# The third chunk's schedule of a hybrid encoder step, written out product by product

## The chip, the cores and the metric

The kernel runs on one core of a Trainium2 chip. A core has five engines, each with a queue of its own: TensorE (PE in the profile; its weight loads are PEld), VectorE (DVE), ScalarE (ACT), GpSimd (POOL) and SyncE (SP), which here does nothing but issue DMA transfers. An engine takes the instructions of its queue in order, so an instruction that waits holds up everything behind it. A semaphore tells an engine that another one, or a transfer, has finished. The metric is device time in microseconds for one execution, smaller is better; several runs are made, and their median counts.

## The reference

One layer of an encoder is applied to 1024 prompt frames and 32 sample frames, with model width 1024. With `rmsnorm` ahead of each part, and residual adds:

1. Mixers: `z = rmsnorm(x) @ w_in` is cut into q, k, v, three convolution inputs and two gates. One mixer is sliding-window attention with 16 heads, the other a gated convolution of width 3. `x += (sigmoid(ga) * (attn @ w_attn_out) + sigmoid(gb) * (conv @ w_conv_out)) @ w_mix_out`.
2. Cross attention with 4 heads into 256 memory tokens: `x += attn(rmsnorm(x) @ w_cq, K_mem, V_mem) @ w_co`.
3. MLP with hidden width 4096: `x += relu(rmsnorm(x) @ w_up)**2 @ w_down`, then a last `rmsnorm`.

The outputs are the two activations and the new key, value, convolution and memory states. Everything is in fp32.

## The kernel before

**Number format.** Each fp32 operand is split into a high part and a low part of a type that TensorE reads fast: ScalarE casts the high part, VectorE subtracts to get the low part (`split`, lines 128 to 130). A product is then three matmuls: high by high, high by low, low by high (`gemm`, L193 to L195; `product`, L864 to L866, for one half of the contraction). Weights come as tiles of 128 x 1024 (512 KB): `fetch_w` (L155) loads one, `issue_w` casts and splits it, two weights ahead of their use. For a weight whose key is in `kept`, the low half is stored to DRAM at the first use (`wl_d`, L172) and loaded at the next ones (L166) in place of the subtraction.

**Chunks and halves.** Features lie on partitions, frames along the free axis. Parts 1 and 2 treat the 1056 frames in three chunks of 384, 384 and 288. The MLP treats them in two halves of 528, each of two quarters of 264, and uses a scheme with seven products in place of eight for 2 x 2 blocks; so it needs sums and differences of weight blocks and of activation blocks. A first part of the MLP's up product, the "first-half products" (`up_one` for one quarter, `up_two` for both), needs only the first half of the frames: `xa[0]` for quarter 0 and `xa[1]` for quarter 1, the latter with its last 144 frames from the second chunk.

**Order of work.** The program is a list, `plan`, of items: functions with the weights that they take. A tile scheduler then orders the instructions on each engine by a timeline that it simulates; those marked `pin` keep their order. The main stages are: 32 hosts (input projections, each with a unit of window attention beside it, `hosts`), the attention output products (`do_attn_out`), the gates (`gate_pair`), then for each chunk eight `do_conv_out` and eight `do_mix` products with the steps of cross attention beside them, then the MLP.

**Sums of weights.** `sum_step` (L702) works on a list of 50 pieces. A step issues from GpSimd's queue the load of one piece (L712, L714) into one of two tiles in turn (`ws`, `xacc`), adds the blocks of the piece of the step before (four additions, L719), and stores the result to DRAM (L723, L725). All of it is pinned. Before the change a step goes with the hosts 3, 5, 7, 9, 11 and each from 12 on (25 steps), one with the first gate, three with each of the eight attention output products. `after_gates` gives the room of `ws` to the tiles M of the merged mixers. `do_conv_out` adds on GpSimd (L1050) after a multiplication on VectorE (L1049); its work tiles and many others share six `ct` slots.

**The third chunk.** The product list of the third chunk (`trunks[2]`, 16 products) runs with the statistics of the first chunk's MLP norm, the cross attention of the second chunk (`cross_steps(1)`: `mem_load_s`, statistics, the query products `do_cq`, six lists of head work from `cross_units`, the output products `do_co`) and `normed(0, f)` beside it, spread by `beside` with one step behind each product. Behind it comes `open_first`, which opens on the room of the M tiles the pool with the Z slots and the `lt` slots. A second list of 32 items follows: `up_one` for weights 0 to 5 in quarter 0, the same in quarter 1, and twenty halves of `up_two`; `then(i, ...)` puts steps behind item i of it. `normed(c, f)` (L1278) makes one normed block and stores it to DRAM (`xn_d`, L1281); `second_load` (L1299) fetches quarter 1 from there, `second_split` (L1293, L1294) splits it. `chunk_col` and `chunk_row` make the norm's statistics as a column and as a row R.

**The activation sums.** `open_sums` loads 16 raw blocks from `xn_d`. `comb_sums(k)` (L1371 to L1383), for k from 0 to 3, forms differences in `xacc`, copies them over the raw blocks by DMA, and splits `t2`. `up_ready` loads sums of weights into the tiles `s31` and `s24`. `up_start` and 16 times `up_pair` follow; in the first `up_pair` the blocks b22 and n4 are split (`comb_split`) before the difference `h22` (L1477).

Of the kernel before, what the change touches and what calls it, by code (L numbers as in the profile page):

```python
# [18 lines left out]
P = 128  # L19
# [21 lines left out]
def hybrid_step(ctx: ExitStack, tc: tile.TileContext, io):  # L41
# [693 lines left out]
    for i, h in enumerate(hosts):  # L735
# [278 lines left out]

    m_cm = mpool = cr_cm = cr = None

    def after_gates():
# [201 lines left out]

    L, S = {}, {}  # L1220
# [33 lines left out]
    def zslot(dt=F32R):  # L1254
        return S["z"].tile([P, HT], dt, tag="Z", bufs=8, name=nm("Z"))

    def lslot(dt=F32):
        return S["z"].tile([P, HT], dt, tag="lt", bufs=6, name=nm("lt"))

# [16 lines left out]
    def normed(c, f):  # L1276
        t = tmp(CH[c][1])
        pin(dve.scalar_tensor_tensor(t, x1[c][f], col(G_MLP + f), R[c], op0=ALU.mult, op1=ALU.mult))  # L1278
        for h, to, at in in_halves(c):
            if c < 2 or f > 3:  # L1280
                sp.dma_start(xn_d[h][:, f, to], t[:, at])  # L1281
        if c == 2:
            sp.dma_start(raw("n1" if f < 4 else "n3", f % 4)[:, HT - CH[c][1] :], t)
# [6 lines left out]
    def split_here(hi, lo):  # L1290
# [16 lines left out]
    def put(*args):  # L1307
        later.append(args)
# [6 lines left out]
    def up_one(i, q):  # L1315


        def fn(w):
            flush()
            a, b = (acc_tile([P, QT]) for _ in range(2))  # L1320
            s, h = lslot(), lslot()
            product(a, w, 0, xa[q][:4], True)
            s, h = s[:, :QT], h[:, :QT]
            act.copy(s, a)
            put(quarter(s1_d[:, i], q), s)
            product(b, w, 1, xa[q][4:], True)
            dve.tensor_add(h, b, s)
            dve.scalar_tensor_tensor(h, h, 0.0, h, op0=ALU.max, op1=ALU.mult)
            put(quarter(op_d["b11"][:, i], q), h)
# [40 lines left out]

    def comb_sums(k):  # L1371
        n3, n1 = xacc[0][:, :HT], xacc[0][:, HT:]
        t2 = L["pool"].tile([P, 1024], F32, tag="wr2", bufs=2, name=nm("t2"))[:, :HT]
        pin(dve.tensor_sub(n3, raw("n1", k), raw("n3", k)))
        sp.dma_start(raw("n3", k), n3)
        pin(dve.tensor_sub(t2, raw("t2", k), n3))
# [3 lines left out]
        pin(act.copy(hi, t2))  # L1380
        pin(dve.tensor_sub(lo, t2, hi.bitcast(F32)))
# [79 lines left out]
    def up_pair(i):  # L1461
# [18 lines left out]
        squared_relu(h22)  # L1480
        put(op_d["b22"][:, i], h22)
        if last:
            pump2(4)
# [147 lines left out]
    normeds = lambda c, at: [(at + f, lambda f=f: normed(c, f)) for f in range(NF)]  # L1631
    left = beside(left + cross_steps(1), trunks[2], normeds(0, 2))
    assert not left
# [12 lines left out]
    call = lambda fn, *args: lambda: item(lambda: fn(*args))  # L1646
    then(0, call(chunk_col, 1))
    then(1, call(chunk_row, 1), call(chunk_col, 2))
    for f in range(NF):
        then(2 + f // 4, call(normed, 1, f))  # L1650
    then(2, call(chunk_row, 2))
    then(3, lambda: item(do_cq(2, 0), ("w_cq", 0)))
    then(4, lambda: item(do_cq(2, 1), ("w_cq", 1)))
    for f in range(NF):
        then(4, call(second_load, f))
        then(5, call(second_split, f))
    for i, (_, calls) in zip((5, 7, 9, 10, 12, 14, 15), cross_units(2)):
        then(i, *[call(x) for x in calls])
    then(16, call(open_sums))
    then(17, lambda: item(do_co(2, 0), ("w_co", 0)))  # L1660
    then(18, lambda: item(do_co(2, 1), ("w_co", 1)))
    then(19, call(open_late), call(chunk_col, 2))
    then(20, call(chunk_row, 2))
    then(21, call(xacc_tile))
    for f in (0, 4, 1, 5, 2, 6, 3, 7):
        then(21, call(normed, 2, f))
    for k in range(4):
        then(23 + k, call(comb_sums, k))
    then(27, call(up_second, 0))
    then(28, call(comb_split, "n1"))  # L1670
    assert len(fillers) == 32
    for i, filler in enumerate(fillers):
# [273 lines left out]
```

## Time and profile before

| | |
|---|---|
| median of 3 runs | 1784.36 us (1780.86 to 1791.03) |
| the profiled execution | 1793.09 us, its span 1791.3 us |
| TensorE busy | 1735.8 us (97%) |
| VectorE, ScalarE, GpSimd busy | 1175.1, 853.9, 580.5 us |
| mean granted TensorE clock | 0.988 |
| SyncE's DMA queue, GpSimd's DMA queue | 306.32 MB, 52.60 MB |
| HBM read, written | 257.08 MB, 97.34 MB |

The span runs from the first to the last instruction. Views are told by what they are: the page has the totals, 40 slices of the span with busy tenths, and the costliest groups; the windows view has the busy time of each engine in chosen stretches; the waits view has who waited for whom; the view in order of time has start, duration, engine, line, operation, output and inputs, and in brackets the idle time before and what ended it. An engine's name with a q behind it is its sequencer, which issues DMAs.

### The profile page before, as it was taken

What the parts mean: (1) busy time and instruction counts of PE and PEld (TensorE: products, weight loads), DVE (VectorE), ACT (ScalarE), POOL (GpSimd) and SP (SyncE); (2) the same over time, 40 slices, a digit from 0 to 9 for tenths busy, and PEclk for the clock granted to TensorE, in tenths of its full rate; (3) what the DMA queues carried; (4) which work ended last, traced back from release to release, by engine and by line L of the source; (5) the groups of instructions that cost most, each with busy time, mean ns of one, the idle gap of its engine ahead of it and who ended that gap; (6) DMA issues with size and microseconds to landing.
All of it is one profiled execution on the core that took longest, in us unless ns stands there. A gap on an engine that the chain in (4) does not pass through costs nothing.

```text
span 1791.3 us, 32530 instructions
## 1 busy us (share of the span) xinstructions
PE 1735.8 (97%) x12250; PEld 1717.5 (96%) x12250; DVE 1175.1 (66%) x2221; ACT 853.9 (48%) x1646; POOL 580.5 (32%) x655
## 2 busy tenths in 40 slices
PE   8999999999999999997999988999999999999998
PEld 8999999999999999996899987999999999999998
DVE  6776767868666747554667775557666686556575
ACT  8643534435345334333556664655444463433443
POOL 0023145653453444453215140014555510100121
PEclk9999999999999999998999999998999999999999
DMA  5332234344346888766765768787766686554554
GB/s 181 101 112 92 87 104 153 118 145 144 134 151 239 289 297 279 269 239 239 245 230 193 251 241 290 254 289 237 228 220 221 214 297 218 179 187 167 191 176 159
DMA packets 186684, 360.98 MB, mean 202 GB/s; under 512 B 19216, under 2 KB 103984, under 8 KB 186400
## 3 DMA queue, kind: packets, MB, share of 16 engines
q1 hardware_dynamic: 171472, 306.32, 50.6%
q0 software_dynamic: 15056, 52.60, 8.2%
q8 instruction: 96, 1.57, 0.4%
q14 instruction: 60, 0.49, 0.1%
HBM read 257.08 MB, written 97.34 MB: 198 GB/s over the span
## 4 chain that ended last, share of the span: by engine, by line
PE 73%; DMA 13%; POOL 7%; DVE 3%; issue 2%; ACT 1%; SPq 0%; DVEq 0%; ACTq 0%; POOLq 0%
PE acc L193 10%; PE acc L195 10%; PE acc L194 10%; PE acc L1733 6%; PE acc L1732 6%; PE acc L1731 6%; DMA wsum_d<-ws 3%; PE acc L864 3%; PE acc L866 3%; PE acc L865 3%; DMA wsum_d<-xacc 3%; POOL ws L719 3%; POOL xacc L719 3%; PE pc L866 2%; PE pc L865 2%
## 5 line engine op out<-in xcount | busy, mean ns | idle before, releaser
L129 ACT CAST wh<-wr 128x1024 fp32r<-128x1024 f32 x217 | 227.8, 1050 | 415.9 <-PE acc L1732 125.7
L130 DVE TENSOR_TENSOR wl<-wr,wh 128x1024 fp32r<-128x1024 f32 x217 | 283.3, 1306 | 143.3 <-ACT wh L129 142.0
L193 PE MATMUL acc<-X,wh 128*128 128x384 f32 (+1 forms) x864 | 282.3, 327 | 7.6 <-ACT wh L129 7.6
L194 PE MATMUL acc<-X,wh 128*128 128x384 f32 (+1 forms) x864 | 279.4, 323 | 0.0
L195 PE MATMUL acc<-X,wl 128*128 128x384 f32 (+1 forms) x864 | 278.8, 323 | 0.3 <-DVE wl L130 0.3
L269 POOL TENSOR_TENSOR xacc<-xacc,ct 128x384 f32<-128x384 f32 (+1 forms) x56 | 74.1, 1328 | 414.2 <-ACT ct L267 404.2
L193 PEld LDWEIGHTS acc<-X,wh 128*128 128x128 f32 x864 | 163.2, 189 | 8.3 <-ACT wh L129 7.6
L194 PEld LDWEIGHTS acc<-X,wh 128*128 128x128 f32 x864 | 163.6, 189 | 0.6
L195 PEld LDWEIGHTS acc<-X,wl 128*128 128x128 f32 x864 | 163.1, 189 | 0.9 <-DVE wl L130 0.8
L193 PE MATMUL acc<-Y,wh 128*128 128x384 f32 (+1 forms) x432 | 139.9, 326 | 12.8 <-DVE ct L1049 12.8
L195 PE MATMUL acc<-Y,wl 128*128 128x384 f32 (+1 forms) x432 | 140.0, 325 | 3.2 <-DMA wl<-wl_d 3.1
L194 PE MATMUL acc<-Y,wh 128*128 128x384 f32 (+1 forms) x432 | 140.0, 325 | 0.6 <-DVE Y L775 0.6
L1733 PE MATMUL acc<-n,wl 128*128 128x264 f32 x352 | 100.0, 284 | 0.0
L1731 PE MATMUL acc<-n,wh 128*128 128x264 f32 x352 | 100.0, 284 | 0.0
L1732 PE MATMUL acc<-n,wh 128*128 128x264 f32 x352 | 100.0, 284 | 0.0
L129 ACT CAST PTh<-pt 128x512 fp32r<-128x512 f32 (+3 forms) x94 | 46.1, 517 | 109.5 <-PE pt L582 107.5
L719 POOL TENSOR_TENSOR ws<-ws 128x256 f32<-128x256 f32 x100 | 94.2, 942 | 5.7
L193 PEld LDWEIGHTS acc<-Y,wh 128*128 128x128 f32 x432 | 81.5, 189 | 13.2 <-ACT wh L129 13.1
L719 POOL TENSOR_TENSOR xacc<-xacc 128x256 f32<-128x256 f32 x100 | 86.9, 869 | 5.5
L195 PEld LDWEIGHTS acc<-Y,wl 128*128 128x128 f32 x432 | 81.6, 189 | 4.2 <-DMA wl<-wl_d 3.7
L194 PEld LDWEIGHTS acc<-Y,wh 128*128 128x128 f32 x432 | 81.6, 189 | 1.1 <-DVE Y L775 1.1
L864 PE MATMUL acc<-n,wh 128*128 128x264 f32 x256 | 72.7, 284 | 1.0 <-DVE Z L1477 1.0
(398 smaller groups left out, 5512.2 us busy)
## 6 DMA issues: line engine op xcount, KB each, us to landing
wr<-in_w_in SPq DMA_DIRECT2D x53, 512.0 KB, 4.0
wr<-in_w_up SPq DMA_DIRECT2D x52, 512.0 KB, 4.9
wr<-wsum_d SPq DMA_DIRECT2D x40, 512.0 KB, 3.4
wl<-wl_d SPq DMA_DIRECT2D x26, 512.0 KB, 4.8
wr<-in_w_conv_out SPq DMA_DIRECT2D x24, 512.0 KB, 4.3
wr<-in_w_mix SPq DMA_DIRECT2D x24, 512.0 KB, 4.2
wr<-in_w_down SPq DMA_DIRECT2D x24, 512.0 KB, 3.7
n_d<-Z SPq DMA_DIRECT2D x32, 264.0 KB, 4.6
```

What stands on the lines that cost most here:

```text
L129: act.copy(hi, src)
L130: dve.tensor_sub(lo, src, hi.bitcast(F32))
L193: pe.matmul(out, wh[:, a], hi, start=(k == 0), stop=False)
L194: pe.matmul(out, wh[:, a], lo, start=False, stop=False)
L195: pe.matmul(out, wl[:, a], hi, start=False, stop=(k == len(acts) - 1))
L719: pin(pool_e.tensor_tensor(t[:, to], t[:, x], t[:, y], op=ALU.add))
L864: pe.matmul(acc, wh[:, a], hi, start=(start and k == 0), stop=False, skip_group_check=True)
L865: pe.matmul(acc, wh[:, a], lo, start=False, stop=False, skip_group_check=True)
L866: pe.matmul(acc, wl[:, a], hi, start=False, stop=(k == 3), skip_group_check=True)
L1731: pe.matmul(a, wh[:, s], hi, start=(t == 0 and k == 0), stop=False, skip_group_check=True)
L1732: pe.matmul(a, wh[:, s], lo, start=False, stop=False, skip_group_check=True)
L1733: pe.matmul(a, wl[:, s], hi, start=False, stop=(t == 1 and k == 7), skip_group_check=True)
```

## The change

Six things change.

- Hosts 4, 6, 8 and 10 get a `sum_step` too (29 steps in the host stage).
- The two lists become one of 48 items: 0 to 7 the third chunk's `do_conv_out`; then its eight `do_mix` with first-half products of quarter 0 at items 10, 13 and 16 between them; 19 to 21 the other three of quarter 0; 22 to 27 those of quarter 1; 28 to 47 `up_two`. All steps beside them are written out with `then`, and `open_first` stands behind item 18, the last mix product. The first three first-half products take their results' tiles from the cross pool.
- The low halves of the six `w_up` weights are no longer kept in DRAM, and for the third chunk neither are those of `w_cq` and `w_co`: VectorE computes them.
- Quarter 1's operands: `second_load` is gone. `open_first` loads the 120 frames of the first chunk from `xn_d`, and `normed(1, f)` copies the 144 frames of the second chunk from its tile.
- `comb_sums` becomes `sums_first` and `sums_then`, the second called one item later; k = 1 uses the tiles `s31` and `s24`, and `up_ready(0)` follows behind it.
- In the first `up_pair`, the splits of b22 and n4 go behind the stores of `h22` and of the last product.

```diff
-        if i % 2 and i > 1 or i > 11:
+        if i % 2 and i > 1 or i > 3:
             extras.append((1, sum_step))
...
     def open_first():
         closed(m_cm)
-        S["z"] = ctx.enter_context(tc.tile_pool(name="first", bufs=1, reuse_waits="tile"))
+        S["l"] = ctx.enter_context(tc.tile_pool(name="first", bufs=6, reuse_waits="tile"))
+        S["z"] = ctx.enter_context(tc.tile_pool(name="second", bufs=8, reuse_waits="tile"))
+        for f in range(NF):
+            z = zslot()
+            xa[1][f] = (quarter(z, 0), quarter(z, 1))
+            sp.dma_start(xa[1][f][1].bitcast(F32)[:, : CH[0][1] - QT], xn_d[0][:, f, QT : CH[0][1]])
+        for name in ("w_cq", "w_co"):
+            del kept[name, 1]
...
     def open_late():
...
-        up_ready(0)
...
     def normed(c, f):
...
+        if c == 1:
+            sp.dma_start(xa[1][f][1].bitcast(F32)[:, CH[0][1] - QT :], t[:, : HT - CH[1][0]])
...
-    def second_load(f):
-        z = zslot()
-        xa[1][f] = (quarter(z, 0), quarter(z, 1))
-        sp.dma_start(xa[1][f][1].bitcast(F32), xn_d[0][:, f, QT:])
...
     def up_one(i, q):
...
-            s, h = lslot(), lslot()
+            if q == 0 and i < 3:
+                s, h = (cr.tile([P, QT], F32, tag=t, bufs=2, name=nm(t)) for t in ("us", "uh"))
+            else:
+                s, h = lslot()[:, :QT], lslot()[:, :QT]
...
-    def comb_sums(k):
-        n3, n1 = xacc[0][:, :HT], xacc[0][:, HT:]
+    def sums_first(k):
+        if k == 1:
+            n3, n1 = (L["pool"].tile([P, 1024], F32, tag=t, name=nm(t))[:, :HT] for t in ("s31", "s24"))
+        else:
+            n3, n1 = xacc[0][:, :HT], xacc[0][:, HT:]
...
+        pin(act.copy(comb["t2", k][0], t2))
+
+    def sums_then(k):
+        t2 = t2s.pop(k)
         hi, lo = comb["t2", k]
-        pin(act.copy(hi, t2))
         pin(dve.tensor_sub(lo, t2, hi.bitcast(F32)))
...
-        if i == 0:
-            comb_split("b22")
-            comb_split("n4")
         h22 = lt()
...
         put(op_d["b22"][:, i], h22)
+        if i == 0:
+            comb_split("b22")
...
+        if i == 0:
+            comb_split("n4")
         if not last:
             m2 = sums()
...
-    left = beside(left + cross_steps(1), trunks[2], normeds(0, 2))
-    item(open_first)
-    kept.update((("w_up", UP[i][0]), None) for i in range(NQ))
-    fillers = [up_one(i, q) for q in range(2) for i in range(NQ)]
+    ones_q = [up_one(i, q) for q in range(2) for i in range(NQ)]
+    mixes = trunks[2][NF:]
+    fillers = trunks[2][:NF] + mixes[:2]
+    for i in range(3):
+        fillers += [ones_q[i]] + mixes[2 * i + 2 : 2 * i + 4]
+    fillers += ones_q[3:]
...
+    then(0, *[call(x) for x in left[0][1]], call(mem_load_s))
+    then(1, call(chunk_stats, 1))
+    then(2, *[lambda j=j: item(do_cq(1, j), ("w_cq", j)) for j in range(2)])
     for f in range(NF):
+        then(2 + f, call(normed, 0, f))
+    for i, (_, calls) in zip((3, 5, 7, 9, 11, 12), cross_units(1)):
+        then(i, *[call(x) for x in calls])
+    then(14, lambda: item(do_co(1, 0), ("w_co", 0)))
+    then(15, lambda: item(do_co(1, 1), ("w_co", 1)))
+    then(16, call(chunk_col, 1))
+    then(17, call(chunk_row, 1))
+    then(18, call(open_first))
     for f in range(NF):
+        then(19 + f // 4, call(normed, 1, f))
+        then(21, call(second_split, f))
+    then(19, call(chunk_col, 2))
+    then(20, call(chunk_row, 2))
+    then(21, lambda: item(do_cq(2, 0), ("w_cq", 0)))
+    then(22, lambda: item(do_cq(2, 1), ("w_cq", 1)))
+    for i, (_, calls) in zip((23, 24, 26, 27, 29, 30, 31), cross_units(2)):
...
+    then(32, call(open_sums))
...
+    then(35, call(open_late), call(chunk_col, 2))
...
     for k in range(4):
-        then(23 + k, call(comb_sums, k))
+        then(39 + k, call(sums_first, k), *([call(sums_then, k - 1)] if k else []))
+    then(41, call(up_ready, 0))
+    then(43, call(sums_then, 3), call(up_second, 0))
+    then(44, call(comb_split, "n1"))
```

More of the change, by code (lines that the diff above doesn't have):

```diff
@@ L1015, in hybrid_step @@
     m_cm = mpool = cr_cm = cr = None
+    L, S = {}, {}
     def after_gates():
@@ L1254, in zslot @@
     def zslot(dt=F32R):
-        return S["z"].tile([P, HT], dt, tag="Z", bufs=8, name=nm("Z"))
+        return S["z"].tile([P, HT], dt, tag="Z", name=nm("Z"))
     def lslot(dt=F32):
-        return S["z"].tile([P, HT], dt, tag="lt", bufs=6, name=nm("lt"))
+        return S["l"].tile([P, HT], dt, tag="lt", name=nm("lt"))
     def lt():
@@ L1369, in second_b22 @@
             sp.dma_start(raw("b22", k), xn_d[1][:, k + 4])
-    def comb_sums(k):
-        n3, n1 = xacc[0][:, :HT], xacc[0][:, HT:]
-        t2 = L["pool"].tile([P, 1024], F32, tag="wr2", bufs=2, name=nm("t2"))[:, :HT]
+    t2s = {}
+    def sums_first(k):
[3 more added lines that the diff above has]
+            n3, n1 = xacc[0][:, :HT], xacc[0][:, HT:]
+        t2 = t2s[k] = L["pool"].tile([P, 1024], F32, tag="wr2", bufs=2, name=nm("t2"))[:, :HT]
         pin(dve.tensor_sub(n3, raw("n1", k), raw("n3", k)))
@@ L1646, in hybrid_step @@
     call = lambda fn, *args: lambda: item(lambda: fn(*args))
-    then(0, call(chunk_col, 1))
-    then(1, call(chunk_row, 1), call(chunk_col, 2))
+    assert len(left) == 1
+    then(0, *[call(x) for x in left[0][1]], call(mem_load_s))
+    then(1, call(chunk_stats, 1))
+    then(2, *[lambda j=j: item(do_cq(1, j), ("w_cq", j)) for j in range(2)])
     for f in range(NF):
-        then(2 + f // 4, call(normed, 1, f))
-    then(2, call(chunk_row, 2))
-    then(3, lambda: item(do_cq(2, 0), ("w_cq", 0)))
@@ L1653, in hybrid_step @@
-    then(4, lambda: item(do_cq(2, 1), ("w_cq", 1)))
-    for f in range(NF):
-        then(4, call(second_load, f))
-        then(5, call(second_split, f))
-    for i, (_, calls) in zip((5, 7, 9, 10, 12, 14, 15), cross_units(2)):
-        then(i, *[call(x) for x in calls])
[L1659 to L1664, printed above, removed]
+        then(2 + f, call(normed, 0, f))
@@ L1665, in hybrid_step @@
+    then(21, lambda: item(do_cq(2, 0), ("w_cq", 0)))
+    then(22, lambda: item(do_cq(2, 1), ("w_cq", 1)))
+    for i, (_, calls) in zip((23, 24, 26, 27, 29, 30, 31), cross_units(2)):
+        then(i, *[call(x) for x in calls])
+    then(32, call(open_sums))
+    then(33, lambda: item(do_co(2, 0), ("w_co", 0)))
+    then(34, lambda: item(do_co(2, 1), ("w_co", 1)))
+    then(35, call(open_late), call(chunk_col, 2))
+    then(36, call(chunk_row, 2))
+    then(37, call(xacc_tile))
     for f in (0, 4, 1, 5, 2, 6, 3, 7):
-        then(21, call(normed, 2, f))
+        then(37, call(normed, 2, f))
@@ L1667, in hybrid_step @@
     for k in range(4):
-        then(23 + k, call(comb_sums, k))
-    then(27, call(up_second, 0))
-    then(28, call(comb_split, "n1"))
-    assert len(fillers) == 32
+        then(39 + k, call(sums_first, k), *([call(sums_then, k - 1)] if k else []))
+    then(41, call(up_ready, 0))
+    then(43, call(sums_then, 3), call(up_second, 0))
+    then(44, call(comb_split, "n1"))
+    assert len(fillers) == 48
     for i, filler in enumerate(fillers):
```

5 lines of the change are left out of this document (2 added, 3 removed).

## The prediction

> **What bounds the kernel now.** I read the page first, then the windows, then TensorE's waits, then the queues of the engines that those waits name. From the page: the span, TensorE's slices and its clock.
>
> ```profile
> span 1791.3 us, 32530 instructions
> ...
> PE   8999999999999999997999988999999999999998
> ...
> PEclk9999999999999999998999999998999999999999
> ```
>
> TensorE is busy in nearly every slice, so it is the bound. The change neither adds nor removes a matrix product. It can only win back time in which TensorE sat idle or ran at a lower granted clock, which the digits put around the middle. The windows give the size (span of the stretch, then busy time and instruction count of TensorE, its weight loads, VectorE, ScalarE and GpSimd, then granted clock, DMA share, GB/s):
>
> ```profile
> 200.00:350.00 150.00, 150.00 (x968) 147.82 (x967) 108.92 (x277) 66.84 (x167) 70.21 (x101) 1.00 0.35 118
> 350.00:480.00 130.00, 130.00 (x842) 128.10 (x841) 94.85 (x234) 54.49 (x137) 69.44 (x107) 1.00 0.41 140
> 816.00:828.70 12.70, 0.00 (x0) 0.02 (x1) 2.10 (x5) 2.29 (x4) 7.71 (x12) 0.62 0.43 153
> 828.70:835.00 6.30, 6.23 (x24) 5.73 (x25) 4.70 (x7) 2.79 (x5) 2.76 (x2) 0.68 0.91 309
> 980.00:990.00 10.00, 10.00 (x78) 10.00 (x78) 5.88 (x12) 6.79 (x11) 4.87 (x5) 1.00 0.63 223
> 1034.90:1065.10 30.20, 25.08 (x161) 23.00 (x159) 24.65 (x41) 19.15 (x39) 17.11 (x17) 1.00 0.63 223
> 1065.10:1116.00 50.90, 43.08 (x302) 41.63 (x303) 28.32 (x64) 25.83 (x51) 1.00 (x2) 0.90 0.86 286
> 1150.00:1170.00 20.00, 18.01 (x129) 17.30 (x127) 6.92 (x12) 10.93 (x23) 3.84 (x4) 0.91 1.04 382
> 1170.00:1206.00 36.00, 36.00 (x299) 36.00 (x297) 20.36 (x35) 19.71 (x42) 3.98 (x3) 1.00 0.77 266
> 1204.60:1232.00 27.40, 21.48 (x142) 20.82 (x141) 21.71 (x31) 15.20 (x25) 4.82 (x5) 0.81 0.75 267
> ```
>
> I count as lost what is missing from busy time, plus the missing share of the clock over the stretch. Five places result. A, 816 to 835: 12.7 + 0.32 x 6.3 = 14.7 us. B, 1035 to 1065: 30.2 - 25.1 = 5.1. C, 1065 to 1116: 7.8 + 0.10 x 50.9 = 12.9. D, 1150 to 1170: 2.0 + 1.8 = 3.8. E, 1205 to 1232: 5.9 + 5.2 = 11.1. Together 47.6 us. All else here runs full. The waits name the reasons (who waited for what: total us, times, longest):
>
> ```profile
> PE acc L193 <- DVE ct L1049: 15.1, 3, 12.8
> PE acc L864 <- ACT Z L1293: 4.4, 2, 3.8
> PE acc L864 <- ACT lt L1354: 4.2, 1, 4.2
> PE acc L195 <- DMA wl<-wl_d: 3.1, 2, 1.6
> PE acc L864 <- ACT wh L167: 1.8, 1, 1.8
> PE acc L1204 <- DMA wl<-wl_d: 1.7, 1, 1.7
> PE acc L864 <- DVE Z L1477: 1.0, 1, 1.0
> ```
>
> **Part A: four sum steps go earlier.** The host condition gives every host from 4 on a `sum_step`: four more (hosts 4, 6, 8, 10). All 50 pieces and their order stay. So 29 instead of 25 pieces are taken in the host stage, and the queue behind it is four shorter. What that queue does, GpSimd in order of time, and one ScalarE line:
>
> ```profile
> 551.71 0.68 POOL L714 DMA_DIRECT2D ws<-in_w_down  x1
> 560.98 0.54 POOL L714 DMA_DIRECT2D xacc<-in_w_down  x1 [4.01 <-DMA wsum_d<-xacc]
> ...
> 823.98 1.00 POOL L1050 TENSOR_TENSOR ct<-ct,ct 128x384 f32<-128x384 f32 x1
> 803.39 0.56 DVE L1049 TENSOR_TENSOR ct<-acc,Ga 128x384 f32<-128x384 f32 x1 [0.89 <-PE acc L195]
> 826.06 0.51 ACT L129 CAST M<-ct 128x384 fp32r<-128x384 f32 x1 [17.83 <-DMA usum_d<-ws]
> ```
>
> Each step's load waits in GpSimd's queue until the store of the same buffer has landed. 25 steps fill 551.7 to 824.0, 10.9 us each, long after the program issued them. The first conv_out addition (L1050) needs GpSimd at 804 and stands behind the rest until 824. Meanwhile the six `ct` slots stay taken, and the merged tile M waits for the last sum's store. This is the 12.8 us wait. Four steps fewer end the queue 4 x 10.9 = 44 us sooner, near 780: before 804. What is late next are the m1 loads behind the pump's loads; of the 15.1 us on L1049 the two later waits, 15.1 - 12.8 = 2.3, stay, and I leave 1.2 more of the 14.7 for such a wait. Gain 13.5. The cost lies in the host stage: there a step adds GpSimd work beside the convolution's scalings. The windows at 200 (steps in every other host, then in each) and 350 (in each) show TensorE full all the same. So zero is the nearest row; in the rival below stands what it would cost without that cover.
>
> **Part B: products between mix products.** Three first-half products (24 matmuls of 264 columns, 36.0/299 = 0.12 us each, 2.9 us) go to items 10, 13 and 16: 8.7 us of TensorE work between the last heads of the second chunk. `mem_load_s` joins `chunk_stats(0)` behind item 0, so the second chunk's statistics and heads start one product sooner; its co products stay behind items 14 and 15. VectorE gets three splits and two short operations each, and it was at 24.65 of 30.2 us already:
>
> ```profile
> 1131.09 1.22 DVE L130 TENSOR_TENSOR wl<-wr,wh 128x1024 fp32r<-128x1024 f32 x1
> 1068.60 0.43 DVE L1327 TENSOR_TENSOR lt<-acc,lt 128x264 f32<-128x264 f32 x1 [0.84 <-PE acc L866]
> ```
>
> 3 x (1.22 + 0.43 + 0.43) = 6.2, so 30.9 of 25.1 + 8.7 = 33.8 us: tight. Bounds: all 5.1 back, or 5 us worse if VectorE is late again. I take 3.0, nearer to the first, because those two heads' chains of latency, not VectorE's total, leave the gaps.
>
> **Part C: the second half's operands.** Before, xn goes to DRAM and back (`second_load`); now 120 columns come from DRAM at item 18 and 144 by a copy out of the normed tile.
>
> ```profile
> 1064.40 1.47 DVE L1206 TENSOR_TENSOR Gb<-acc,Gb 128x384 f32<-128x384 f32 x3
> 1078.09 0.48 ACT L252 COPY R<-pr 128x384 f32<-128x384 f32 x1 [0.80 <-PE pr L242]
> 1080.87 3.71 SPq L1281 DMA_DIRECT2D xn_d<-ct  x8
> 1086.45 5.78 SPq L1281 DMA_DIRECT2D xn_d<-ct  x8
> 1102.56 2.22 ACT L1293 CAST Z<-Z 128x264 fp32r<-128x264 f32 x6 [1.25 <-DMA Z<-xn_d]
> wl_d<-wl SPq DMA_DIRECT2D x4, 512.0 KB, 4.1
> Z<-xn_d SPq DMA_DIRECT2D x8, 132.0 KB, 5.6
> n<-ct SPq DMA_DIRECT2D x8, 144.0 KB, 2.3
> xn_d<-ct SPq DMA_DIRECT2D x8, 72.0 KB, 2.9
> ```
>
> Old chain: end of the second chunk's co at 1065, its row R 13.5 us later, stores, loads, splits done near 1104.5: 39 us. New chain: 13.5, then 24 issues on SyncE (8 x 2 stores, 8 copies; 5.78/8 = 0.72 us each crowded, 3.71/8 = 0.46 free; I take 0.46, as the loads that crowded them are gone) with some 9 other issues between them, 15 us, a landing (an SBUF copy took 2.3, a 72 KB store 2.9: I take 2.5, ends 1.6 and 5.6), one split 0.9: 32 us to the last tile, some 5 us less to the first four, which start the product. TensorE's cover: item 16 to 21 holds four half products (11.6) and two mixes (24 matmuls at 10/78 = 0.128, 3.1 each), the column sums (some 3), and a query product (3.1): 24. The next query product can slip in. So a wait of 0 to 8 us stays, with a lower clock behind it. I leave 4.0 of 12.9. On the other side the low halves of six up weights are no longer stored and fetched (6 x 512 KB out, 6 in), nor w_cq's and w_co's fetched (2): 7 MB fewer in stretches at a DMA share of 0.86 and 1.04; this ends the 1.8 us wait on L167, and one of the two of 1.6 on `wl_d`. VectorE takes eight more splits, 9.8 us, of which six fall at items 22 to 27 beside the third chunk's heads; it was busy 28 of 51 us in this window. Gain 8.9, bounds +12.9 and -5. The eight loads of item 18 wait for M slots, so SyncE stands until the last mix product; weights are two ahead (5.8 us), which hides it; without that cover every 512 KB load behind comes 5 us late.
>
> **Part D.** The co product's wait (1.7, L1204) was for its low half behind the sixteen loads of `open_sums`; a split of 1.22 us takes its place. 3.0 of 3.8.
>
> **Part E: sums in two steps.** One `xacc` serves every k, so each round waits for its stores:
>
> ```profile
> 1186.97 0.70 DVE L1374 TENSOR_TENSOR xacc<-n,n 128x528 f32<-128x528 f32 x1
> ...
> 1204.35 0.95 DVE L1374 TENSOR_TENSOR xacc<-n,n 128x528 f32<-128x528 f32 x1 [1.07 <-DMA n<-xacc]
> 1206.14 0.63 ACT L1380 CAST t<-t 128x528 fp32r<-128x528 f32 x1 [2.43 <-DVE t L1376]
> ```
>
> 17.4 us for four, and the last copy (L1380) holds ScalarE's queue before the relu that frees the accumulator (L1354): the 4.2 us wait. With k = 1 in two other tiles, one of three store waits goes, some 5 us, so the relu is hardly late. `up_ready(0)` moves behind k = 1, because it fills the same tiles; SyncE may wait there for those stores, under 5 us, with 20 us to go. The splits of b22 and n4 go behind the first h22, whose subtraction (L1477, 1.0 us of wait) they delayed; then b22 itself is the late one, about 4 x 0.7 us of VectorE against one product of 2.9. I take 6.1 of 11.1, bounds +11.1 and -3.
>
> **The clock.** In the windows it falls to 0.91 at D, where the waits named are 1.7 us long. The Trainium skill, "TensorE: Matmul & The Clock Gate", section on HAM oscillation, gives as abstract rule that no idle gap over about 3.4 us should occur. By that rule D would lose only its 2.0 us of idle time; the trace has shorter waits cost clock too, and I go by the trace.
>
> The Trainium skill, "DMA: Bandwidth & Descriptors", Specifications, says that below 512 B a transfer does read-modify-write. The eight new loads have 120 x 4 = 480 B per partition. No run here shows the price; it speaks against C alone.
>
> **The sum.** 13.5 + 3.0 + 8.9 + 3.0 + 6.1 = 34.5. The profiled execution took 1793.09 us (span 1791.3 and 1.8 around it): 1758.6. It stands 0.5% above the median of the runs, 1784.36 (ratio 0.9951), so 1750. 0.5%, 8.9 us, is about what can be told from no change.
>
> **Rivals.** First: only A pays, the written order opens as many waits as it closes. For it: VectorE at 91% in B, and a chain of 32 us against 24 of cover in C. Against it: the DMAs removed and the third sum wait are simply gone. 1793.1 - 13.5 = 1779.6, in runs 1771. Second: A does not pay, because another wait stands where GpSimd's stood (weights: a DMA share of 0.91 in 828.7 to 835). Against it: after the wait eight products followed with only the 2.3 us named. 1793.1 - 21.0 = 1772.1, 1763. Third, slower: GpSimd bounds the host stage. A step is 10.9 us, the scalings some 3, a host 14.3. If a step with its four transfers needed 13 us, 28 hosts would each last 1.7 longer, +48 - 34.5: 1806, 1797 in runs; it decides from 14.3 + 34.5/28 = 15.5 us per host. Against it, before the change, GpSimd waits for VectorE, not the other way round:
>
> ```profile
> POOL Ga L622 <- DVE Ga L621: 46.1, 14, 9.6
> ```
>
> Fourth: neither A nor the rest moves anything net, 1784.
>
> **Chances.** Forecast 0.60, only A 0.20, only the rest 0.08, slower host stage 0.04, nothing net 0.08 (0.06 within, 0.02 beyond the bound). Faster 0.88, same 0.06, slower 0.06. The range reaches from all 47.6 us back, 1745.5 or 1737, to only A, 1771, with a microsecond or two at either end.
>
> **What would show it.** A: GpSimd's last sum step before 790 and no wait over 3 us between 800 and 835; wrong if TensorE waits there for anything 10 us long, or if the windows at 200 and 350 are no longer full. B: no co product waiting for Y or Ga. C: first product on Z after a wait under 4 us, no `Z<-xn_d` of 132 KB. D: no wait on `wl_d` in the third chunk. E: three, not four, rounds spaced by `n<-xacc`, wait on L1354 under 2 us. The prediction fails above all if C or E opens a wait past 5 us, since the clock doubles part of it.

## The result and the profile after

The changed kernel took 1787.36 us (median of 20 runs, 1781.81 to 1792.44), the kernel before, on the same chip, 1784.41 (20 runs, 1775.05 to 1795.67). The ratio is 1.0013, 95% interval 0.9997 to 1.0029: no change. The forecast was 1750, with a range that ended a microsecond or two above 1771. The profiled execution after took 1787.72 us, the one before 1793.09; so these two traces differ by 5.4 us the other way, and the reason for that is the first thing the experiments settle.

The page of the changed kernel (TensorE's slices and granted clock in tenths), the same rows as at the head of the prediction:

```profile
PE   8999999999999999999999997998999999999998
...
PEclk9999999999999999999999998999999999999999
```

The window of 816 to 835 no longer shows; the low slices now lie at 1070 to 1120 and 1205 to 1250. The windows view of the changed kernel, cut at the places that correspond to those of before (span, then busy time and count of TensorE, its weight loads, VectorE, ScalarE, GpSimd, then granted clock, DMA share, GB/s):

```profile
200.00:350.00 150.00, 150.00 (x966) 147.84 (x965) 110.65 (x278) 66.04 (x164) 79.79 (x113) 1.00 0.38 129
...
780.00:835.00 55.00, 55.00 (x326) 55.00 (x326) 32.66 (x51) 23.60 (x40) 8.74 (x9) 1.00 0.71 245
1000.00:1049.20 49.20, 43.69 (x288) 41.16 (x287) 39.84 (x75) 30.48 (x65) 15.91 (x16) 0.97 0.63 211
1049.20:1076.00 26.80, 26.79 (x201) 26.57 (x201) 18.12 (x38) 12.87 (x25) 3.77 (x4) 0.94 0.61 197
1076.00:1118.00 42.00, 32.70 (x211) 29.07 (x212) 25.00 (x48) 20.50 (x41) 0.00 (x0) 0.88 0.61 205
1118.00:1155.00 37.00, 35.49 (x285) 34.59 (x284) 22.61 (x54) 26.14 (x73) 3.88 (x4) 1.00 0.60 204
1155.00:1195.00 40.00, 40.00 (x320) 40.00 (x318) 21.29 (x35) 24.10 (x50) 3.40 (x2) 0.96 0.76 268
1195.00:1250.00 55.00, 45.02 (x316) 42.66 (x315) 41.29 (x51) 24.53 (x37) 21.97 (x14) 0.91 0.63 228
```

By the prediction's way of counting (missing busy time, plus the missing share of the clock over the stretch), the five places read:

| place | lost before | lost after, with its working | forecast to remain |
|---|---|---|---|
| A, host stage's end | 14.7 | 0 (780 to 835 full) | 1.2 |
| B, second chunk's heads | 5.1 | 5.5 + 0.03 x 49.2 = 7.0 | 2.1 |
| C, first products on Z | 12.9 | 0.06 x 26.8 + 9.3 + 0.12 x 42 = 15.9 | 4.0 |
| D, third chunk's co | 3.8 | 1.5 + 0.04 x 40 = 3.1 | 0.8 |
| E, activation sums | 11.1 | 10.0 + 0.09 x 55 = 15.0 | 5.0 |

A went as said. D lost its wait, but the clock falls behind it all the same (0.96 from 1155 to 1195), so it gains 0.7 us in this trace and not 3.0. B, C and E lose more than before. TensorE's waits in the changed kernel, largest first, with the one on L1203, which is the third chunk's co:

```profile
PE acc L193 <- ACT wh L129: 11.0, 3, 7.6
PE acc L865 <- DVE t L1393: 4.1, 1, 4.1
PE pc L864 <- ACT b L1300: 2.8, 1, 2.8
PE acc L193 <- DVE Ga L1065: 2.3, 1, 2.3
PE acc L864 <- ACT Z L1300: 2.0, 5, 0.6
...
PE acc L1203 <- ACT Y L1185: 1.1, 1, 1.1
PE acc L864 <- DVE Gb L1207: 1.0, 1, 1.0
```

Of the first row, 7.6 us stand at the program's start, as in the kernel before; 3.1 us are new and belong to C. None of the old waits of this stretch is among the first (L1049's 12.8, `Z` of L1293 with 3.8, `lt` of L1354 with 4.2, `wl_d` at L1204 with 1.7). New ones stand at neighbouring instructions of the same products.

**A.** GpSimd in order of time, changed kernel:

```profile
780.19 1.45 POOL L723 DMA_DIRECT2D usum_d<-ws  x2 [0.41 <-POOL ws L719]
802.86 1.00 POOL L1051 TENSOR_TENSOR ct<-ct,ct 128x384 f32<-128x384 f32 x1 [21.22 <-DMA mkr<-mk_d]
```

The last sum is stored at 780 instead of 822, and GpSimd is idle for 21 us before conv_out's first addition needs it (it takes that addition at 803, before at 824). The prediction said "near 780"; the host windows, 200 to 350 and 350 to 480, stayed full.

**C.** SyncE's queue, then ScalarE, then TensorE of the changed kernel, in order of time:

```profile
1068.92 0.85 SPq L1286 DMA_DIRECT2D xn_d<-ct  x2
1069.82 0.52 SPq L1288 DMA_DIRECT2D Z<-ct  x1
...
1082.37 0.47 SPq L1288 DMA_DIRECT2D Z<-ct  x1
...
1083.52 0.43 SPq L155 DMA_DIRECT2D wr<-in_w_cq  x1
```

```profile
1084.23 0.41 ACT L1300 CAST Z<-Z 128x264 fp32r<-128x264 f32 x1 [1.25 <-DMA Z<-ct]
1087.99 1.04 ACT L129 CAST wh<-wr 128x1024 fp32r<-128x1024 f32 x1 [3.35 <-DMA wr<-in_w_cq]
```

```profile
1089.08 0.61 PE L193 MATMUL acc<-Y,wh 128*128 128x288 f32 x1 [3.12 <-ACT wh L129]
```

Each block costs SyncE three issues, two stores and one copy, so one Z tile comes every 1.6 us and the product on Z takes its operands at that pace. The load of `w_cq` stands behind all 24 and is issued at 1083.5; ScalarE, and then TensorE, wait for it. No single wait on Z is long: most of what C loses are the small waits between, the 3.1 us behind them, and the clock that falls with them (0.55 between 1082 and 1093).

**E.** VectorE, then TensorE of the changed kernel at the sums:

```profile
1197.28 0.71 DVE L1385 TENSOR_TENSOR t<-t,xacc 128x528 f32<-128x528 f32 x1 [2.01 <-DMA n<-t]
1198.52 1.32 DVE L1393 TENSOR_TENSOR t<-t,t 128x528 fp32r<-128x528 f32 x2
```

```profile
1199.28 0.59 PE L865 MATMUL acc<-t,wh 128*128 128x264 f32 x1 [4.06 <-DVE t L1393]
...
1213.99 0.81 PE L864 MATMUL pc<-b,wh 128*128 128x264 f32 x2 [2.75 <-ACT b L1300]
```

The store that holds a round is no longer that of `xacc`, but the one that frees `t2` (`n<-t`). The low half of the third `t2` is the first of the two L1393. In VectorE's order it stands behind the first step of the fourth round, which waits for that store, so it comes late and TensorE waits for it. The split of b22, moved behind the squared ReLU, holds the product on b.

### The profile page after: what moved, and what is told of

The parts are those of the page before. It is cut to its first block, busy times and chain, and to the rows that moved or that the text cites. A ratio compares the mean times of both kernels' runs of the same rounds, so it can differ in the third digit from the quotient of the medians.

```text
span 1785.9 us, 32537 instructions
## 1 busy us (share of the span) xinstructions
PE 1738.8 (97%) x12250; PEld 1717.8 (96%) x12250; DVE 1181.0 (66%) x2229; ACT 852.5 (48%) x1646; POOL 584.3 (33%) x655
## 5 line engine op out<-in xcount | busy, mean ns | idle before, releaser
L129 ACT CAST wh<-wr 128x1024 fp32r<-128x1024 f32 x225 | 236.3, 1050 | 435.8 <-PE acc L1758 126.2
L130 DVE TENSOR_TENSOR wl<-wr,wh 128x1024 fp32r<-128x1024 f32 x225 | 293.1, 1303 | 153.1 <-ACT wh L129 152.1
L193 PE MATMUL acc<-X,wh 128*128 128x384 f32 (+1 forms) x864 | 281.8, 326 | 7.6 <-ACT wh L129 7.6
L193 PEld LDWEIGHTS acc<-X,wh 128*128 128x128 f32 x864 | 162.9, 189 | 8.3 <-ACT wh L129 7.6
L193 PE MATMUL acc<-Y,wh 128*128 128x384 f32 (+1 forms) x432 | 139.8, 325 | 3.2 <-ACT wh L129 3.1
L193 PEld LDWEIGHTS acc<-Y,wh 128*128 128x128 f32 x432 | 81.6, 189 | 3.8 <-ACT wh L129 3.4
```

The costliest lines, as they stand in the source:

```text
L129: act.copy(hi, src)
L130: dve.tensor_sub(lo, src, hi.bitcast(F32))
L193: pe.matmul(out, wh[:, a], hi, start=(k == 0), stop=False)
```

## The experiments

**The four sum steps alone.** The kernel before with one line of the change:

```
-        if i % 2 and i > 1 or i > 11:
+        if i % 2 and i > 1 or i > 3:
```

> The kernel before with part A alone: four sum steps more in the host stage. Theory 1 (the 12.8 us wait in the trace of before is one draw of a wait that changes from execution to execution, and is some 6 us in the middle): 4 to 10 us faster than before, ratio 0.994 to 0.998, and runs that lie closer together than those of before (before spread over 20.6 us in 20 runs). Theory 2 (the wait is paid in full in every execution, and the third chunk loses as much): 13 to 15 us faster, ratio 0.992. Both: GpSimd's last sum step ends near 780 us and no wait over 3 us stands between 800 and 835.

Measured: 1779.97 us, ratio to the kernel before 0.9950 (0.9924 to 0.9976). The same kernel, with a trace:

> The kernel before with the four added sum steps alone, once more, as the measure for the combination beside it and for a trace of its own. Both theories: ratio 0.993 to 0.998 to the kernel before; in the trace the last sum step ends before 790 and no wait above 3 us stands between 800 and 835.

Measured: 1779.83 us, ratio 0.9951 (0.9924 to 0.9978), no wait above 1 us from 790 to 875. As theory 1 said, its runs lie closer together: 12 of them within 9.6 us (1776.39 to 1785.94), the 35 of the kernel before beside them within 22.6. Step A alone gives 0.5%, 8.8 us of the 13.5 forecast, and the changed kernel, which has it, is slower than it.

**All but the sum steps.** The changed kernel with the old condition:

```
-        if i % 2 and i > 1 or i > 3:
+        if i % 2 and i > 1 or i > 11:
```

> The changed kernel with the old host condition: all but part A. Theory 1: 6 to 12 us slower than before, ratio 1.003 to 1.007, with the wait at the first conv_out products as in before. Theory 2: 13 to 15 us slower, ratio 1.008.

Measured: 1805.63 us, ratio 1.0088 (1.0058 to 1.0117), which is theory 2's number. The rewrite of the third chunk, forecast to gain 21 us (B to E), costs 0.9% by itself. Beside the sum steps it costs less: the changed kernel's own ratios, 1.0013 here and 1.0003 below, against 0.9951 for the sum steps alone, make it 0.5 to 0.6%, 9 to 11 us. The other 5 to 6 us are probably the old wait. The profiled execution (1804.72 us) pays it in full, 12.9 us at the first conv_out products. Against the two executions of the kernel before that paid it too (1793.09 us above, 1795.53 below) it is 9 to 12 us longer, as much as beside the sum steps. If the median of this kernel holds the whole wait and that of the kernel before a part of it, the difference is explained; why this kernel should pay it more often isn't shown.

**The kernel before, in two further executions.** Nothing is edited.

> The kernel before, unchanged, for a second profiled execution. Theory 1: the wait at L1049 near 816 us and its total time differ from the first trace (12.8 us, 1793.1 us) together, by 4 us or more in one of two such looks. Theory 2: 12 to 13.5 us again, and the total time within 3 us of the first.

> The kernel before, unchanged, for a third profiled execution; the same expectations as for the second.

Measured: 1782.04 and 1795.53 us. GpSimd in order of time, first the 1782.04 us execution, then the 1795.53 us one:

```profile
796.59 1.46 POOL L712 DMA_DIRECT2D ws<-in_w_up  x2 [2.91 <-DMA usum_d<-ws]
...
811.63 1.03 POOL L1050 TENSOR_TENSOR ct<-ct,ct 128x384 f32<-128x384 f32 x1
```

```profile
810.99 1.46 POOL L712 DMA_DIRECT2D ws<-in_w_up  x2 [7.18 <-DMA usum_d<-ws]
...
822.67 1.00 POOL L1050 TENSOR_TENSOR ct<-ct,ct 128x384 f32<-128x384 f32 x1
```

TensorE behind them, in the same order:

```profile
816.26 0.41 PE L193 MATMUL acc<-Y,wh 128*128 128x384 f32 x1 [1.38 <-DVE ct L1049]
```

```profile
827.40 0.66 PE L193 MATMUL acc<-Y,wh 128*128 128x384 f32 x1 [11.55 <-DVE ct L1049]
```

The same program reached conv_out with GpSimd's queue free at 811.6 once and at 822.7 and 824.0 the other times, and TensorE's wait was 1.4 us instead of 11.6 and 12.8. The executions differ by 11.05 us (1793.09 - 1782.04), the waits by 11.4. That the two agree so closely is in part luck: with the clock, which falls beside the long wait, 800 to 850 loses 5.9 us in the short execution (50 - 45.58, plus 0.03 x 50) and 19.9 in the long one (50 - 37.15, plus 0.14 x 50), so some 3 of these 14 us are lost again elsewhere. So the wait that the prediction priced is drawn anew in each execution: each of the 25 steps waits for a store, as the last of them here for 2.9 us and there for 7.2, and the end of the queue comes soon or well after conv_out first needs it. The median of the kernel before contains part of it, the profiled execution all.

**The sums in one step again.** Only the two-step form is undone; the second step follows the first at once.

```
-        then(39 + k, call(sums_first, k), *([call(sums_then, k - 1)] if k else []))
+        then(39 + k, call(sums_first, k), call(sums_then, k))
...
-    then(43, call(sums_then, 3), call(up_second, 0))
+    then(43, call(up_second, 0))
```

This run and the next three share their runs of the kernel before; first the changed kernel as it is, as their measure.

> The changed kernel as it is, as the measure for the three kernels beside it. Both theories: within 0.3% of its first measurement, a ratio between 0.999 and 1.004 to the kernel before; the waits of the profiled execution at the sums (a product on the first t2 tile that waits 4 us near 1199) and at the first products on Z (one every 1.6 us near 1080) are seen again, since nothing in them depends on a store that lands late.

Measured: 1790.87 us (1787.83 to 1794.76), ratio 1.0003 (0.9974 to 1.0032), the waits as in its first trace.

> Only the two-step form of the sums is undone: the second step of round k follows its first step in the same place, so that each of the two buffers of t2 is free one product earlier; everything else is the changed kernel. Theory 'buffers of t2' (the second step holds a buffer for one more product, the next round then waits for its store, and the last store of n lands late): the 4.1 us wait near 1199 and the 8.6 us idle of ScalarE near 1207 go, 4 to 7 us are gained on the changed kernel, ratio to it 0.996 to 0.998. Rival 'one queue' (the stores and the loads of the sums crowd SyncE's queue whichever way the steps are cut): within 2 us of the changed kernel, the wait only moves.

Measured: 1785.46 us, ratio 0.9979 (0.9957 to 1.0001): 5.4 us less than the changed kernel by the medians, with 12 runs from 1780.62 to 1790.27. TensorE's waits from 1150 to 1250, first of the changed kernel's repeat, then of the one-step form:

```profile
PE acc L865 <- DVE t L1393: 4.8, 1, 4.8
PE pc L864 <- ACT b L1300: 2.8, 1, 2.8
```

```profile
PE pc L864 <- ACT b L1300: 4.3, 1, 4.3
PE acc L864 <- ACT lt L1347: 2.9, 1, 2.9
PE acc L864 <- ACT lt L1358: 1.8, 1, 1.8
```

The time is as the theory of the buffers said, the mechanism only in part. VectorE still waits for the store of a `t2`:

```profile
1189.07 0.71 DVE L1385 TENSOR_TENSOR t<-t,xacc 128x528 f32<-128x528 f32 x1 [3.65 <-DMA n<-t]
```

What went is the wait on the low half (L1393), which now follows its round at once instead of a product later. ScalarE's copies hold its reads of the accumulators again (2.9 and 1.8 us), and the split of b costs 4.3 us. The two profiled executions (1787.83 and 1786.67 us) differ by 1.2 us only, so these rows show what moved at the sums, not where the whole 5.4 us come from.

**The stores on GpSimd's queue.**

```
         for h, to, at in in_halves(c):
             if c < 2 or f > 3:
-                sp.dma_start(xn_d[h][:, f, to], t[:, at])
+                (pool_e if c == 1 else sp).dma_start(xn_d[h][:, f, to], t[:, at])
```

> The 16 stores of the second chunk's normed columns (xn_d<-ct) are issued from GpSimd's queue instead of SyncE's; the copies into Z stay on SyncE's. Theory 'SyncE's issue rate' (24 issues in a row at about 0.5 us, one Z tile every 1.6 us): Z tiles come every 0.6 us, the products on Z near 1080 follow each other without waits, the load of w_cq is issued 8 us earlier and the wait of 3.1 us behind it goes; 5 to 8 us gained on the changed kernel, ratio 0.9955 to 0.997. Rival 'the chain's length' (statistics, R and the splits come too late by themselves, cover 27 us between the end of co and the first product on Z): the first product on Z waits instead, once and longer, and the time stays within 2 us of the changed kernel.

Measured: 1786.74 us, ratio 0.9990 (0.9970 to 1.0010): 4.1 us less than the changed kernel by the medians, a little under what was expected. SyncE, then TensorE, then the window, in this kernel:

```profile
1071.68 2.50 SPq L1288 DMA_DIRECT2D Z<-ct  x4
...
1076.27 1.51 SPq L155 DMA_DIRECT2D wr<-in_w_cq  x1
```

```profile
1080.44 0.39 PE L864 MATMUL acc<-Z,wh 128*128 128x264 f32 x1 [2.06 <-ACT Z L1300]
```

```profile
1076.00:1093.00 17.00, 12.68 (x89) 11.41 (x89) 12.47 (x28) 9.32 (x21) 4.60 (x9) 1.00 0.80 254
```

The first copies follow each other in 0.6 us, `w_cq` is issued 7 us earlier, the wait of 3.1 us behind it is gone, and the row of small waits is one of 2.1 us. The clock stays at 1.00 there, where it was 0.55 between 1082 and 1093 in the changed kernel. So SyncE's rate of issue did bound this place; behind it the chain is still 2 us late. Not all that the issues saved was won: the median landing of the copies is 4.9 us here, where it was 1.8 in the changed kernel. The Trainium skill, "DMA: Bandwidth & Descriptors", section "Issuing engines are not separate DMA queues", says that issuing from several engines only saves the issuing sequencer's time, usually small beside the transfer. The trace agrees on what is saved; 24 issues in 13.9 us (1068.92 to 1082.84) were not small here beside a landing of 1.8 us.

**The mix products first.**

```
-    fillers = trunks[2][:NF] + mixes[:2]
-    for i in range(3):
-        fillers += [ones_q[i]] + mixes[2 * i + 2 : 2 * i + 4]
+    fillers = trunks[2] + ones_q[:3]
```

> Only the order of 9 fillers is undone: the three first-half products stand behind the last mix product again instead of between them; the items of attention, statistics and loads keep their numbers. The cover between the end of co and the first product on Z stays the same within 1 us (two mix products of 3.5 us leave it, two first-half products of 3.2 us join it). Theory 'the products between the mixes made waits of their own' (the gate tiles Ga and Gb come late for a first-half product's neighbour: 2.3, 0.7, 0.6 and 1.0 us in the profile): these waits go, 2 to 5 us gained. Rival, the forecast's step B (they cover the waits of co): 1 to 4 us lost, the waits for Y before the co products come back.

Measured: 1795.08 us, ratio 1.0033 (1.0012 to 1.0054): 4.2 us more than the changed kernel by the medians. The windows of the changed kernel's repeat, then of this kernel:

```profile
1000.00:1050.00 50.00, 43.94 (x297) 40.94 (x296) 40.03 (x75) 30.64 (x67) 15.09 (x16) 1.00 0.64 210
...
1200.00:1250.00 50.00, 43.78 (x314) 42.30 (x314) 38.92 (x46) 21.25 (x30) 21.31 (x14) 0.91 0.61 210
```

```profile
1000.00:1050.00 50.00, 43.40 (x302) 40.99 (x301) 39.04 (x77) 31.46 (x67) 14.37 (x15) 1.00 0.65 215
...
1200.00:1250.00 50.00, 41.69 (x271) 39.00 (x272) 38.34 (x45) 23.74 (x37) 17.66 (x11) 0.86 0.65 231
```

The rival's sign and size came out, but not at its place: in the heads (1000 to 1050) the two orders lose alike, other waits replacing those for Ga and Gb, and most of the difference in these two traces stands at the sums, 150 us later. Nothing was edited there, and how the order of the mixes reaches the sums isn't shown. That the products between the mixes cover the heads is therefore not shown either; only that this order is not the part that loses.

**The sums wholly as before**, with the added sum steps and the third chunk as changed: the old `comb_sums` on `xacc` alone, `up_ready(0)` in `open_late`, and

```
         doubled(banks_of(B[i]), wset[i, 3], 0, "n3", False)
+        if i == 0:
+            comb_split("b22")
+            comb_split("n4")
         h22 = lt()
```

> Step E undone whole: one-step sums in the buffers of before, the loads of the ready sums and the splits of b22 and n4 at their old places; A, B, C and D as changed. Theory 'E loses by all of its edits' (the t2 buffers, and the b22 split, which now starts only behind the squared ReLU and holds the products 2.8 to 4.3 us): 6 to 9 us gained on the changed kernel (median of it 1787 to 1791), the waits for b and n near 1210 to 1216 go, the wait of 4.2 us for the lt of L1354 of the kernel before comes back. Rival 'only the buffers of t2': the same 5 us as the one-step form alone.

Measured: 1782.83 us, ratio 0.9977 (0.9951 to 1.0002). Against the changed kernel that is 8.0 us by the medians (1790.87), which were taken at different times, and 4.6 by the ratios (1.0003), whose intervals overlap. With the 5.4 us of the one-step form, which was measured beside the changed kernel, E costs some 5 to 8 us. TensorE's waits from 1150 to 1250:

```profile
PE acc L864 <- ACT lt L1359: 1.6, 1, 1.6
```

This one comes first; in this trace none for b is left, and for n none either. The old wait of 4.2 us on `lt` came back as 1.6 only (L1359 is L1354 of before), so that expectation was too high. Whether the late split of b costs more than the one-step form showed can't be told: 2.6 us between medians taken at different times is within the spread of the runs.

**The same with the stores on GpSimd's queue**, the two edits together:

> The same, and the second chunk's stores of xn_d on GpSimd's queue. Theory 'each part has its own loss': the two gains add up, 10 to 13 us on the changed kernel, about 1777, the ratio to the kernel before 0.992 to 0.996, level with the added sum steps alone or 3 us ahead of them. Rival 'the rewrite of the third chunk loses elsewhere' (its products between the mixes, clock): 1781 to 1784, behind the sum steps alone.

Measured: 1779.22 us (1770.53 to 1783.08), ratio 0.9945 (0.9917 to 0.9973); beside it the sum steps alone gave 1779.83. The gains add up as the first theory said, and both kernels are beaten. But it ends level with one line of the change. The stretch 980 to 1250, sum steps alone first, then this kernel:

```profile
980.00:1250.00 270.00, 250.71 (x1859) 245.73 (x1858) 179.77 (x326) 159.39 (x324) 57.05 (x47) 0.96 0.77 257
```

```profile
980.00:1250.00 270.00, 248.60 (x1847) 241.72 (x1846) 188.14 (x340) 158.87 (x326) 64.38 (x63) 0.96 0.69 227
```

With both faults mended, the rewritten stretch is nearly as full as the old one (2.1 us less, at the same clock), with a lower DMA share (0.69 against 0.77) and more on VectorE (188 against 180 us). The transfers that B, C and D took away bought no time here. Some waits at the sums are left: TensorE waits 2.8 us for n in this trace, where the kernel of the experiment above had no such wait.

**The low halves kept**, on the changed kernel:

```
-        for name in ("w_cq", "w_co"):
-            del kept[name, 1]
...
+    kept.update((("w_up", UP[i][0]), None) for i in range(NQ))
```

> Step D undone: the low halves of the first six w_up tiles, of w_cq and of w_co are stored once and loaded again, as in the kernel before; all else as changed. Forecast's step D: 3 us lost against the changed kernel, a wait for wl_d of 1.5 to 2 us at the co products near 1143. Rival (the split made anew costs ScalarE and VectorE what the load cost): within 2 us; a gain of 2 to 4 us if the new splits (the wait of 3 us for wh near 1090 is one of them) hold the products more than the loads did.

Measured: 1789.73 us, ratio 0.9993 (0.9966 to 1.0020), level with the changed kernel (1.0003) within the noise: the 3 us of the forecast's step D don't show, and the median lies on the other side. The trace has no wait on `wl_d` in the third chunk, contrary to step D's reason, but one of another kind (SyncE, then TensorE; between them ScalarE's cast of the weight, L167, waits for the load):

```profile
1085.78 0.59 SPq L155 DMA_DIRECT2D wr<-in_w_up  x1
```

```profile
1091.13 0.59 PE L864 MATMUL acc<-Z,wh 128*128 128x264 f32 x1 [10.11 <-ACT wh L167]
```

The 24 issues stood in front of a weight load again, here the weight of the product on Z itself: the 10.1 us take the place of the small waits, which the same issues cause. It shows again what the store experiment showed. Because this wait is new, the run gives D's sum and not its price at the co products alone.

## Why the prediction was wrong

The sum failed at its terms B to E: 21.0 us of gain forecast, 9 to 11 us of loss measured beside the sum steps. Two steps failed. C counted SyncE's 24 issues up to the last tile, but not that they set the pace of the product on Z and stand in front of a weight load. E counted the stores of `xacc`, but not how long the second step holds a `t2` buffer. With both mended the kernel is 11.7 us faster (1790.87 to 1779.22), which is what the rewrite had cost.

**A was right in its mechanism and too large.** "25 steps fill 551.7 to 824.0" was read from one execution; in another the queue ended at 811.6 and the wait was 1.4 us. The term of 13.5 is right for the profiled execution, which lost 14.7 us there, and is 8.8 in the medians. The scaling by 0.9951 from the profiled execution to the median treated that difference as spread over the whole span, when the wait itself can make it. "No wait over 3 us between 800 and 835" held in every trace with the added steps.

**B, forecast 3.0.** "No co product waiting for Y or Ga" held by its letter only: a co product's wait of 0.6 us and a first-half product's of 1.0 us, both for Gb, and a mix product's wait of 2.3 us for Ga replace them, and the place loses 7.0 instead of 5.1. Undoing the order costs 4.2 us, but elsewhere. The sign holds, the reason given for it isn't shown.

**C, forecast 8.9, is where the reasoning failed first.** The chain was reckoned at 32 us against 24 of cover. It took 35.5 (co's end 1049.2, last tile cast at 1084.7), and the cover was 26.8 (to the first products on Z near 1076): 8.7 us late where 8 was named as the upper end. That was nearly right, and the taken value of 4.0 for the remaining loss was not: the lateness is not one wait but is spread over a product whose operands come every 1.6 us; the clock halves beside it (0.55); and a load that stands behind the 24 issues makes one more wait. "The next query product can slip in" is the line that failed: that product (L193 at 1089.1) waited 3.1 us for its own weight, `w_cq`, issued behind the 24. The first product on Z waited under 4 us, as the list of signs asked, and the place still lost 15.9 us. The sign was too weak. "The loads that crowded them are gone" gave 0.46 us an issue; it was 0.58 on the mean (13.9/24), even with them gone. The eight loads of 480 B per partition, which the prediction could not price, landed in 2.3 us (median, 60 KB each), so no loss from them shows.

**D, forecast 3.0.** The wait on `wl_d` went, and the place reads 3.1 instead of 3.8. Of its old loss 1.8 us were clock, and the clock fell again, behind the third chunk's column sums and with no wait before it; in the changed kernel's repeat it did not fall there. Keeping the halves costs no time that can be told from the noise. The prediction took a wait's length as the price of its cause; with the cause restored the wait did not return, though the loads stood in another order in that trace.

**E, forecast 6.1, measured 5 to 8 us the other way.** "One of three store waits goes": it did, and the others on `xacc` with it; VectorE waits for no `n<-xacc` there any more (before 0.92, 1.85 and 1.07 us at L1374). Left out was the other buffer of the same round. `t2` has two, the second step holds each for a product more, and the low half of `t2` is itself an operand; VectorE makes it only behind the next round's first step. "Wait on L1354 under 2 us" held, and 4.1 us opened one instruction further. "About 4 x 0.7 us of VectorE against one product of 2.9" for b22 missed that ScalarE's part of it comes behind the squared ReLU in its queue.

The rival "only A pays" was the nearest in kind: with the two faults mended it is what remains (1779.2 against 1779.8). Its price for the kernel as written was still too good, because the rewrite does not come out even but costs 9 to 11 us, which is what A gains. The fourth rival, nothing net at 1784 us, has the measured number, but by luck: in its words neither part moves anything, and the runs show A gaining 8.8 us and the rest losing as much. The sentence that the prediction fails "if C or E opens a wait past 5 us" named the places; the waits stayed under 5 us each and did it together with the clock.

## What to carry to other kernels

Before pricing a wait from one trace, ask how near its cause is to not mattering: a queue that ends just after it is needed gives the whole wait in one execution and none in the next, and only the median of several shows what it is worth. When a round trip through DRAM is replaced by copies, count the issues on the queue, not the bytes, and list what loads stand behind them. When a step is cut in two, list every buffer that it holds in between, and which product reads the half that now comes later.

## What the runs showed of the hardware

The granted clock fell without an idle gap. Behind the second chunk's co, TensorE makes 24 recorded matmuls of one column for the column sums, at first between other products and then, for some 2 us, alone. The changed kernel's windows there, then those of the same place in the kernel with both faults mended:

```profile
1052.40:1055.70 3.30, 3.30 (x31) 3.30 (x29) 2.09 (x3) 2.33 (x2) 0.00 (x0) 1.00 0.66 242
1055.70:1059.10 3.40, 3.40 (x16) 3.40 (x16) 0.82 (x5) 0.20 (x1) 0.00 (x0) 0.50 0.60 198
```

```profile
1054.70:1058.00 3.30, 3.30 (x31) 3.30 (x30) 2.09 (x3) 2.33 (x2) 0.00 (x0) 1.00 0.73 263
1058.00:1062.00 4.00, 4.00 (x32) 4.00 (x32) 1.62 (x7) 1.63 (x4) 0.67 (x1) 1.00 0.50 168
```

TensorE is recorded as busy in all four, and in the first execution the 3.4 us behind the sums run at half clock, in the other at full. One kernel shows both, too: behind the third chunk's sums the changed kernel has such a dip (the row of 0.96 from 1155 to 1195, with TensorE busy for all 40 us), and its repeat has 1.00 there. The Trainium skill, "TensorE: Matmul & The Clock Gate", section "HAM oscillation", asks that no idle gap exceed about 3.4 us. By that rule there would be no loss here; the trace has one of 1.7 us, so what a one-column matmul counts as activity seems to matter, which no run here isolates. The length of the slow stretch, 3.4 us, and that it comes in one execution and not in the other, agree with the window of about that length that runs freely, of which the same page's section "What's actually happening" speaks.
